# Up projection of a decoder layer: right sums of twelve pairs formed in HBM by DMA, five pairs by seven products in five chunks, and six u tiles kept in HBM

## The chip, the cores and the metric

The kernel runs on one core of one Trainium2 chip. The metric is the time of one execution in microseconds on the device; for the kernel before it is the median of 3 runs. A profile of one execution shows what each engine did: TensorE (PE; its weight loads apart, PEld), VectorE (DVE), ScalarE (ACT), GpSimd (POOL) and SyncE (SP). SP and GpSimd also issue DMAs; each of the two has an order of its own and stands still at an instruction whose semaphores aren't there yet.

## The reference

One layer of a decoder: 256 tokens, width 2048, eight heads of dilated window attention beside eight heads of latent attention, then an MLP of width 8192. All in float32. The change lies in the up projection:

```python
x = x + _rmsnorm(mixed @ w_out[layer], norm_attn_post[layer])
h = _rmsnorm(x, norm_mlp_pre[layer])
u = jnp.square(jax.nn.relu(h @ w_up[layer]))
x = x + _rmsnorm(u @ w_down[layer], norm_mlp_post[layer])
```

## The kernel before

**Precision.** Each float32 operand is split into a part hi and a rest lo, both in a reduced format that TensorE takes; a product of two operands is three matmuls, hi·hi, hi·lo and lo·hi (`three`). Splitting a weight tile is one ScalarE operation (hi, `L306`, or `L310` where a gain is multiplied in) and one VectorE operation (lo, `L307` or `L311`).

**Stages.** Input projections and attention, output projection, residual and norm, up projection, down projection. Weights stream from HBM: `Weights.emit` loads a 512 KB tile into one of 5 raw buffers (on SP's queue), splits it into one of 8 pairs of hi and lo buffers, and runs 6 tiles ahead of the tile in use.

**The up projection** runs over 8 chunks j of 1024 columns of `w_up`. The depth of 2048 is 16 row blocks of 128. A plain step ("k") multiplies one row block with both halves of the tokens and both halves of the columns: 4 products, 12 matmuls. A step by seven products ("w") takes two row blocks (a pair, number kp) and does the 2 x 2 block product with 7 products in place of 8: 21 matmuls where two plain steps take 24. For that it needs sums of the left blocks (`left_sums`, made once, kept in `late["st"]`) and sums of the right, the weights: with the pair's blocks b11, b12 (upper rows) and b21, b22 (lower rows), t holds b11 + b12 and b12 + b22, u holds b11 + b12 + b22 and that plus b21. VectorE makes t and u from the raw pair (`seven`, `L361`, `L365`, `L366`; about the same from two raw tiles, `L364`); four tiles are then split: b11 alone (512 columns), the lower block b (1024), u and t.

A pair's raw weights come as one DMA of 1 MB on GpSimd's queue into the buffer `ab` or `ab2` (`L374`), or as two raw tiles. `UP_STEPS` holds the steps of each chunk: none by seven products in chunk 0, three in chunks 1 and 7, four in chunks 2 to 6, there with a plain step between any two. The products that go to more than one accumulator are gathered in banks m; `close` adds them up in `c` at the chunk's end (`L1043`), and four adds (`L1109`) put that on the accumulators. Each chunk then gives two u tiles (relu and scale, transpose on TensorE, square): `up_evac`, emitted in the next chunk. The 16 u tiles stay in SBUF until the down projection splits them (`split_u`).

**Order.** Nothing is scheduled at run time: the program writes each engine's instructions in one order. A planner (`Flow`) keeps a clock that advances with each matmul written, and chains (generators) that yield delays; `flow.pump` writes the next piece of every chain that is due. The clock decides only where in the order a piece stands.

**GpSimd's queue before.** From the start to the up projection it holds the small power operations of the norms (`L501`: rstd_pre, rstd_kv, rstd_q, rstd_pw, rstd_post) and two or three fills; then the DMAs of the pairs.

Of the kernel before, what the change touches and what calls it, by code (L numbers as in the profile page):

```python
# [98 lines left out]
UP_PAIRS = [()] + [("ab", "ab2", "ab", "ab2")] * 5 + [("ab2", "ab", "raw", "ab"), ("ab", "raw", "raw")]  # L99
# [11 lines left out]
UP_STEPS = [up_steps(range(16)), THREE] + [FOUR] * 5 + [THREE]  # L111

ST = 13 * 256
# [150 lines left out]
def layer(nc, tc, io):  # L264
# [79 lines left out]
    late = {}  # L344
# [32 lines left out]
    def seven_up(j, kp):  # L377
        def load():
            if UP_PAIRS[j][kp] == "raw":
                return [weights.load(up_weight(j, 2 * kp + i), CW, f"raw_w{j}_{kp}{i}") for i in range(2)]  # L380
            return load_two(late[UP_PAIRS[j][kp]], nc.gpsimd if (j, kp) > (1, 0) else nc.sync,
                            io["w_up"][2 * kp * P:(2 * kp + 2) * P, j * CW:(j + 1) * CW])

        return seven(load, lambda: [late["up"].tile([P, CW], F32, tag="T", bufs=2, name=f"{n}{j}_{kp}") for n in "tu"])
# [32 lines left out]
    for j in range(FF // CW):  # L417
        wide_u.append([])
        for what, k in UP_STEPS[j]:
            if what == "k":  # L420

                ts = [weights.plan(up_weight(j, k), 1, CW, *([gcol[:, 8 + k:9 + k]] if j < 2 or k >= 2 * max(N_SEVEN) else []))]
            else:
# [254 lines left out]
    pre = flow.start(prelude())  # L678
    tab = flow.start(tables())
# [253 lines left out]
    def up_evac(j, b, i, acc, order):  # L933
# [8 lines left out]
        if j not in uT:  # L942
            if j in (0, 1, 10, 11, 12, 13):
                t2 = late["u01" if j < 2 else "ab2" if j < 12 else "ab"][:, j % 2 * CW:(j % 2 + 1) * CW]
            else:
                tag = {"tag": "T", "bufs": 2} if j > 13 else {}
                t2 = late["up"].tile([P, CW], F32, name=f"uT{j}", **tag)
            uT[j] = t2.rearrange("p (k s) -> p k s", k=4)
        nc.scalar.activation(uT[j][:, :, b * P:(b + 1) * P], t.rearrange("p (k s) -> p k s", k=4), AF.Square)

# [32 lines left out]
    def left_sums(kp):  # L983
# [9 lines left out]
        keep = kp >= min(N_SEVEN[1:])  # L993
# [5 lines left out]
        st = [late["st"][:, 768 * kp + i * n:768 * kp + (i + 1) * n] for i in range(2)]  # L999
# [8 lines left out]
        yield 0.5  # L1008

# [11 lines left out]
    def seven_products(ts, left, accs, m, first, last, m_first=False):  # L1021
# [6 lines left out]
        for p, (a, i, half, to) in enumerate(prods):  # L1028
            w = weights.get(ts[i])
            in_m = isinstance(to, int)  # L1030
# [20 lines left out]
    for j in range(FF // CW):  # L1051
# [9 lines left out]
        for t, b in order:  # L1061
            what, k, tiles = steps[t]
            if (j, t, b) == (0, 8, 0):
# [4 lines left out]
                late["st"] = late["up"].tile([P, ST], F32R, tag="st", bufs=1, name="st")  # L1068
                for n in ("ab", "ab2", "c", "u01"):
# [5 lines left out]
            if (j, what, k, b) == (1, "k", 8, 0):  # L1075
# [233 lines left out]
```

## Time and profile before

| | us |
|---|---|
| median of 3 runs (1047.1 to 1048.34) | 1047.68 |
| span of the profiled execution, first to last instruction | 1045.7 |
| TensorE busy in the span | 1035.7 |
| VectorE busy | 838.7 |
| ScalarE busy | 630.4 |
| GpSimd busy | 51.5 |
| HBM read / written | 212.72 MB / 15.73 MB |

The span leaves out what lies before the first and after the last instruction. Busy times are shares of one execution. The profile has several views: the page (busy times, 40 slices, DMA queues, the chain of work that ended last, the costliest groups), groups by line, a timeline, waits, and windows (busy time of each engine in a stretch of time). Times in them count from the span's start. A group names its line, engine, operation, output tile, input tiles and shape. In this execution chunk 1 of the up projection begins at 401.4 us, chunk 2 at 444.7 and the down projection at 701.6.

### The profile page before, as it was taken

The page shows a single profiled execution, that of the slowest core. Times are in us where ns is not written, and L with a number is a line of the kernel's source. Part 1 is how long each engine was busy: PE and PEld are TensorE (multiplying, and loading weights), DVE is VectorE, ACT ScalarE, POOL GpSimd, SP SyncE. Part 2 cuts the span into 40 slices and gives each one's busy share as a digit, 9 for nine tenths or more (in the row PEclk, how much of TensorE's full clock was granted, in tenths as well). Part 3 has the DMA queues.
Part 4 walks back from the last instruction along what each step waited for, and adds up shares of the span by engine and source line. Part 5 has one row for each costly group of instructions (what it writes and reads, how often), then busy time and mean ns, then how long its engine had stood idle before and what let it go on. Part 6 is the DMA issues. An engine that isn't in the chain of part 4 may idle for free.

```text
span 1045.7 us, 13378 instructions
## 1 busy us (share of the span) xinstructions
PE 1035.7 (99%) x4837; PEld 863.2 (83%) x4837; DVE 838.7 (80%) x1122; ACT 630.4 (60%) x848; POOL 51.5 (5%) x83
## 2 busy tenths in 40 slices
PE   9999999999999999999999999999999999999996
PEld 6888889888888888888888888888888888888885
DVE  6676536567557669999999999897899978999995
ACT  6674436565545566665765667666567564766661
POOL 0000000000000000000000000000000000111100
PEclk9999999999999999999999999999999999999998
DMA  9975547454447295646657356378778767698952
GB/s 303 370 229 148 140 129 241 146 162 153 150 156 236 92 360 188 216 147 207 202 185 246 121 201 207 113 253 325 274 276 303 265 232 261 238 332 323 356 204 83
DMA packets 79938, 229.33 MB, mean 219 GB/s; under 512 B 6912, under 2 KB 11520, under 8 KB 79488
## 3 DMA queue, kind: packets, MB, share of 16 engines
q1 hardware_dynamic: 64576, 171.47, 48.9%
q0 software_dynamic: 14864, 56.63, 15.2%
q8 instruction: 38, 0.62, 0.3%
q10 hardware_dynamic: 432, 0.37, 0.1%
q14 instruction: 28, 0.23, 0.1%
HBM read 212.72 MB, written 15.73 MB: 218 GB/s over the span
## 4 chain that ended last, share of the span: by engine, by line
PE 97%; DVE 1%; issue 1%; ACT 0%; POOL 0%; DVEq 0%; POOLq 0%; ACTq 0%
PE y L296 25%; PE acc_u L296 24%; PE acc_o L296 8%; PE m L296 7%; PE md L296 5%; PE acc_qk L296 4%; PE acc_v L296 4%; PE acc_ckv L296 2%; PE acc_ukv L296 2%; PE acc_q L296 2%; PE acc_cq L296 2%; PE acc_k L296 2%; PE acc_uq L296 2%; PE rt L300 1%; PE sc_b L296 1%
## 5 line engine op out<-in xcount | busy, mean ns | idle before, releaser
L307 DVE TENSOR_TENSOR lo<-raw,hi 128x1024 fp32r<-128x1024 f32 (+3 forms) x213 | 241.5, 1152 | 89.8 <-ACT hi L306 89.1
L306 ACT ACTIVATE hi<-raw 128x1024 fp32r<-128x1024 f32 (+3 forms) x213 | 209.9, 999 | 73.6 <-PE y L296 16.1
L296 PE MATMUL y<-hi,uhi 128*128 128x512 f32 x370 | 144.4, 390 | 0.0
L296 PE MATMUL y<-hi,ulo 128*128 128x512 f32 x370 | 144.1, 389 | 0.0
L296 PE MATMUL y<-lo,uhi 128*128 128x512 f32 x370 | 144.0, 389 | 0.0
L296 PE MATMUL acc_u<-hi,hT_hi 128*128 128x512 f32 x356 | 141.7, 398 | 0.0
L296 PE MATMUL acc_u<-hi,hT_lo 128*128 128x512 f32 x356 | 139.2, 391 | 0.4 <-DVE hT_lo L307 0.4
L296 PE MATMUL acc_u<-lo,hT_hi 128*128 128x512 f32 x356 | 138.9, 390 | 0.0
L311 DVE SCALAR_TENSOR_TENSOR lo<-raw,gcol,hi 128x1024 fp32r<-128x1024 f32 x74 | 92.5, 1279 | 9.5 <-ACT hi L310 9.5
L310 ACT ACTIVATE hi<-raw,gcol 128x1024 fp32r<-128x1024 f32 x74 | 83.7, 1148 | 25.0 <-DMA raw<-in_w_up 11.7
L296 PEld LDWEIGHTS y<-hi,ulo 128*128 128x128 f32 x370 | 69.5, 188 | 14.4
L296 PEld LDWEIGHTS y<-lo,uhi 128*128 128x128 f32 x370 | 69.5, 188 | 14.3
L296 PEld LDWEIGHTS y<-hi,uhi 128*128 128x128 f32 x370 | 69.5, 188 | 14.2
L296 PEld LDWEIGHTS acc_u<-hi,hT_lo 128*128 128x128 f32 x356 | 66.8, 188 | 14.9 <-DVE hT_lo L307 0.8
L296 PEld LDWEIGHTS acc_u<-lo,hT_hi 128*128 128x128 f32 x356 | 67.0, 188 | 12.8
L296 PEld LDWEIGHTS acc_u<-hi,hT_hi 128*128 128x128 f32 x356 | 67.0, 188 | 12.8
L306 ACT ACTIVATE hi<-u 128x1024 fp32r<-128x1024 f32 (+1 forms) x38 | 37.4, 990 | 49.2 <-DVE u L366 35.4
L307 DVE TENSOR_TENSOR lo<-st_down,hi 128x1024 fp32r<-128x1024 f32 x42 | 50.4, 1220 | 3.0 <-ACT hi L306 2.8
L296 PE MATMUL acc_o<-hi,mixT_hi 128*128 128x512 f32 x128 | 51.8, 405 | 0.0
L306 ACT ACTIVATE hi<-st_down 128x1024 fp32r<-128x1024 f32 x42 | 43.9, 1052 | 12.6 <-PE y L296 9.5
L296 PE MATMUL acc_o<-hi,mixT_lo 128*128 128x512 f32 x128 | 50.2, 392 | 0.0
L296 PE MATMUL acc_o<-lo,mixT_hi 128*128 128x512 f32 x128 | 50.0, 391 | 0.0
(328 smaller groups left out, 2087.7 us busy)
## 6 DMA issues: line engine op xcount, KB each, us to landing
raw<-in_w_down SPq DMA_DIRECT2D x86, 512.0 KB, 5.8
raw<-in_w_up SPq DMA_DIRECT2D x76, 512.0 KB, 4.6
raw<-in_w_in SPq DMA_DIRECT2D x55, 512.0 KB, 4.9
ab<-in_w_up POOLq DMA_DIRECT2D x22, 1024.0 KB, 5.4
raw<-in_w_out SPq DMA_DIRECT2D x32, 512.0 KB, 4.2
ab_down<-in_w_down POOLq DMA_DIRECT2D x11, 1024.0 KB, 7.1
ukeep<-ulo SPq DMA_DIRECT2D x15, 512.0 KB, 7.0
ulo<-ukeep POOLq DMA_DIRECT2D x15, 512.0 KB, 6.2
```

Of the source, the lines that this page charges most:

```text
L296: nc.tensor.matmul(out, a, b, start=start, stop=stop)
L300: nc.tensor.transpose(out, a, ident)
L306: nc.scalar.activation(hi, src, AF.Copy)
L307: nc.vector.tensor_tensor(out=lo, in0=src, in1=hi.bitcast(F32), op=OP.subtract)
L310: nc.scalar.activation(hi, src, AF.Copy, scale=g)
L311: nc.vector.scalar_tensor_tensor(out=lo, in0=src, scalar=g, in1=hi.bitcast(F32), op0=OP.mult, op1=OP.subtract)
```

## The change

**Right sums by DMA.** `MADE` names twelve pairs (chunk, pair): pair 1 in chunks 1 and 7, pairs 1 and 3 in chunks 2 to 6. A new chain `make_sums`, started at the beginning with a delay of 62 and steps of 4.8 on the planner's clock, writes four DMAs for each on GpSimd's queue, in batches of three pairs: a copy of the pair from `w_up` to a new HBM tensor (1 MB), an add of b12 and b22 onto b11 and b12 (512 KB), an add of b22 onto b21 (256 KB), and an add of the first sum onto the second half (512 KB, from the tensor itself). The adds are DMAs that accumulate. In the up projection these pairs are four ordinary weight tiles on SP's queue (512, 1024, 1024 and 1024 columns; two of them from the made tensor), and VectorE makes no sums for them.

**More pairs.** Chunks 2 to 6 take five pairs in place of four, chunk 7 four in place of three: six pairs more. The steps of chunks 2 to 6 are now blocks 10 to 13, pairs 0, 1, block 14, pairs 2, 3, 4, block 15. A fifth set of left sums is made in chunk 1 (`two_sums`), in a tile `st4`; `late["st"]` shrinks by 256 columns.

**u tiles in HBM.** The raw pairs that aren't made use `ab` and `ab2` alone, through chunk 7 too, so these no longer hold u tiles 10 to 13. The u tiles 2 to 7 are stored to HBM on SP's queue 6 units after they are written (`u_away`, in chunks 2 to 4), their buffers serve tiles 8 to 13, and they are read back: 2 and 3 in chunk 7, 4 to 7 at the start of the down projection.

How this moves instructions on VectorE, in chunk 4, from the splits of pair 2 to the last plain block. Before (lo is the rest of a split tile, t and u the sums of the pair named after them, raw a loaded tile):

```order
L307 TENSOR_TENSOR lo_4964<-ab,hi_4963 128x1024
L307 TENSOR_TENSOR lo_4971<-u_2_4931,hi_4970 128x1024
L307 TENSOR_TENSOR lo_4981<-t_2_4930,hi_4980 128x1024
L361 TENSOR_TENSOR t_3_4991<-ab_3503 128x1024
L365 TENSOR_TENSOR u_3_4992<-t_3_4991,ab_3503 128x512
L366 TENSOR_TENSOR u_3_4992<-u_3_4992,ab_3503 128x512
L311 SCALAR_TENSOR_TENSOR lo_4999<-raw_4996,gcol,hi_4998 128x1024
L307 TENSOR_TENSOR lo_5009<-ab_3503,hi_5008 128x512
L307 TENSOR_TENSOR lo_5025<-ab_3503,hi_5024 128x1024
L307 TENSOR_TENSOR lo_5032<-u_3_4992,hi_5031 128x1024
L307 TENSOR_TENSOR lo_5042<-t_3_4991,hi_5041 128x1024
L311 SCALAR_TENSOR_TENSOR lo_5054<-raw_5051,gcol,hi_5053 128x1024
```

Now, from the splits of pair 3, which is made in HBM, to those of pair 4:

```order
L309 TENSOR_TENSOR lo_5085<-raw_5082,hi_5084 128x512
L309 TENSOR_TENSOR lo_5097<-raw_5094,hi_5096 128x1024
L386 TENSOR_TENSOR t_4_5113<-ab 128x1024
L390 TENSOR_TENSOR u_4_5114<-t_4_5113,ab 128x512
L391 TENSOR_TENSOR u_4_5114<-u_4_5114,ab 128x512
L309 TENSOR_TENSOR lo_5121<-raw_5118,hi_5120 128x1024
L309 TENSOR_TENSOR lo_5130<-raw_5127,hi_5129 128x1024
L309 TENSOR_TENSOR lo_5140<-ab,hi_5139 128x512
L309 TENSOR_TENSOR lo_5150<-ab,hi_5149 128x1024
L309 TENSOR_TENSOR lo_5160<-u_4_5114,hi_5159 128x1024
L309 TENSOR_TENSOR lo_5167<-t_4_5113,hi_5166 128x1024
L313 SCALAR_TENSOR_TENSOR lo_5179<-raw_5176,gcol,hi_5178 128x1024
```

The plain block's split between the pairs is gone, and pair 3 comes as four raw tiles without sums of its own.

GpSimd's queue ahead of the output projection's norms, before (the power operations, and a fill):

```order
L501 TENSOR_TENSOR rstd_kv<-t_kv,neg_half 128x2
L501 TENSOR_TENSOR rstd_q<-t_q,neg_half 128x2
L738 MEMSET krT 128x512
L501 TENSOR_TENSOR rstd_pw<-t_pw,neg_half 128x2
L501 TENSOR_TENSOR rstd_post_3197<-t_post_3196,neg_half 128x1
```

Now, the last batch (made_1_79, made_3_80 and made_1_81 are the tensors of pairs 1 and 3 of chunk 6 and of pair 1 of chunk 7):

```order
L368 DMA made_1_79<-in_w_up 128x2x512
L368 DMA made_1_79<-in_w_up 128x512
L368 DMA made_3_80<-in_w_up 128x2x512
L368 DMA made_3_80<-in_w_up 128x512
L368 DMA made_1_81<-in_w_up 128x2x512
L368 DMA made_1_81<-in_w_up 128x512
L368 DMA made_1_79<-made_1_79 128x2x512
L528 TENSOR_TENSOR rstd_pw<-t_pw,neg_half 128x2
L368 DMA made_3_80<-made_3_80 128x2x512
L368 DMA made_1_81<-made_1_81 128x2x512
L528 TENSOR_TENSOR rstd_post_3257<-t_post_3256,neg_half 128x1
```

Of the 48 new DMAs 20 stand ahead of rstd_kv, 5 between it and rstd_q, 21 between that and rstd_pw, and 2 behind rstd_pw; the adds wait for the copies and for the adds that they build on.

The diff, its core:

```diff
-UP_PAIRS = [()] + [("ab", "ab2", "ab", "ab2")] * 5 + [("ab2", "ab", "raw", "ab"), ("ab", "raw", "raw")]
+MADE = [(), (1,)] + [(1, 3)] * 5 + [(1,)]
+D_MADE, MADE_STEP, MADE_BATCH = 62.0, 4.8, 3
...
-UP_STEPS = [up_steps(range(16)), THREE] + [FOUR] * 5 + [THREE]
-
-ST = 13 * 256
+FIVE = up_steps(range(10, 14), (), (14,), (), (), (15,))
+UP_STEPS = [up_steps(range(16)), THREE] + [FIVE] * 5 + [FOUR]
+
+ST = 12 * 256
...
+    def make_sums():
+
+        jobs, add = [(j, kp) for j in range(FF // CW) for kp in MADE[j]], {"accum_op": OP.add}
+        H = 512
+        yield D_MADE
+        for i in range(0, len(jobs), MADE_BATCH):
+            todo = [[], [], []]
+            for j, kp in jobs[i:i + MADE_BATCH]:
+                s = made[j, kp]
+                w = up_pair(j, kp).rearrange("(k p) n -> p k n", k=2)
+                todo[0].append((s.rearrange("p (k n) -> p k n", k=2), w, {}))
+                todo[1].append((s[:, :CW].rearrange("p (k n) -> p k n", k=2), w[:, :, H:], add))
+                todo[1].append((s[:, CW:CW + H], w[:, 1, H:], add))
+                todo[2].append((s[:, CW:].rearrange("p (k n) -> p k n", k=2), s[:, :H].unsqueeze(1).to_broadcast([P, 2, H]), add))
+            for group in todo:
+                for out, src, kw in group:
+                    nc.gpsimd.dma_start(out=out, in_=src, **kw)
+                    yield MADE_STEP
...
+            elif k in MADE[j]:
+                s = made[j, k] = dram.tile([P, 2 * CW], F32, name=f"made{j}_{k}")
+                ts = [weights.plan(up_weight(j, 2 * k)[:, :512], 1, 512), weights.plan(up_weight(j, 2 * k + 1), 1, CW),
+                      weights.plan(s[:, CW:], 1, CW), weights.plan(s[:, :CW], 1, CW)]
...
     pre = flow.start(prelude())
+    flow.start(make_sums())
...
+        if b and 2 <= j < 8:
+            flow.start(u_away(j), 6.0)
+
+    U_HOME = {2: 8, 3: 9, 10: 4, 11: 5, 12: 6, 13: 7}
+    uaway = {}
+
+    def u_away(j):
+        uaway[j] = dram.tile([P, CW], F32, name=f"uaway{j}")
+        nc.sync.dma_start(out=uaway[j], in_=uT.pop(j).rearrange("p k s -> p (k s)"))
+        yield 0
+
+    def u_back(j, t):
+        nc.sync.dma_start(out=t, in_=uaway[j])
+        uT[j] = t.rearrange("p (k s) -> p k s", k=4)
...
-            if (j, what, k, b) == (1, "k", 8, 0):
-                fourth = flow.start(left_sums(3), 20.0)
-            if j == 2 and t == 0:
-                flow.finish(fourth)
+            if (j, what, k, b) == (1, "k", 10, 0):
+                more_sums = flow.start(two_sums(), 12.0)
+            if (j, what, k) == (1, "w", 2):
+                flow.finish(more_sums)
+            if (j, t, b) == (FF // CW - 1, 6, 0):
+                for i in (2, 3):
+                    u_back(i, late["up"].tile([P, CW], F32, tag=f"k{i}", bufs=1, name=f"uT{i}_back"))
...
+    for i in range(4, 8):
+        u_back(i, late["ab" if i < 6 else "ab2"][:, i % 2 * CW:(i % 2 + 1) * CW])
```

35 lines of the change are left out of this document (22 added, 13 removed).

## The prediction

> **What bounds the kernel now.** I read the page's busy times and chain of waits first, then the chain in time order over the up projection, then VectorE's groups there, then the windows of the DMA engines.
>
> ```profile
> span 1045.7 us, 13378 instructions
> PE 1035.7 (99%) x4837; PEld 863.2 (83%) x4837; DVE 838.7 (80%) x1122; ACT 630.4 (60%) x848; POOL 51.5 (5%) x83
> ...
> PE 97%; DVE 1%; issue 1%; ACT 0%; POOL 0%; DVEq 0%; POOLq 0%; ACTq 0%
> ```
>
> TensorE is busy for 1035.7 of 1045.7 us and is 97% of the chain that ended last. So a matmul taken out shortens the kernel by its own pace, as long as nothing else becomes late. The chain in time order gives that pace (start, length, piece):
>
> ```profile
> 482.78 9.52 PE acc_u L296 x42
> ...
> 520.04 2.72 PE acc_u L296 x12
> 522.76 2.72 PE m L296 x12
> 525.48 9.52 PE acc_u L296 x42
> ```
>
> Twelve products in 2.72 us are 0.2267 us each. The 390 ns that the page gives for one product is its length in the pipeline, not its pace. Chunks start 42.70 us apart (482.78 and 525.48 are the same place in two of them), and 180 products at 0.2267 us are 40.8 us of that; sixteen transposes and their joints are the rest. VectorE stands right behind. Its groups in one chunk (line, operation, shape, count; busy us and mean ns; idle before them):
>
> ```profile
> L311 DVE SCALAR_TENSOR_TENSOR lo<-raw,gcol,hi 128x1024 fp32r<-128x1024 f32 x8 | 9.9, 1279 | 0.0
> L307 DVE TENSOR_TENSOR lo<-t,hi 128x1024 fp32r<-128x1024 f32 x4 | 4.9, 1220 | 0.8 <-ACT hi L306 0.8
> ...
> L361 DVE TENSOR_TENSOR t<-ab 128x1024 f32<-128x1024 f32 x4 | 4.9, 1218 | 0.0
> ...
> L365 DVE TENSOR_TENSOR u<-t,ab 128x512 f32<-128x512 f32 x4 | 2.8, 692 | 0.1
> L307 DVE TENSOR_TENSOR lo<-ab,hi 128x512 fp32r<-128x512 f32 x4 | 2.7, 686 | 0.3 <-ACT hi L306 0.3
> L1043 DVE TENSOR_TENSOR c<-m,c 128x512 f32<-128x512 f32 x4 | 2.7, 688 | 0.2
> L1109 DVE TENSOR_TENSOR acc_u<-acc_u,c 128x512 f32<-128x512 f32 x4 | 2.5, 692 | 0.0
> ```
>
> ```profile
> 444.68:487.38 42.70, 42.70 (x198) 35.35 (x196) 40.87 (x44) 28.08 (x33) 2.85 (x4) 1.00 0.62 203
> ```
>
> The second row is the same chunk as a window: TensorE 42.70 of 42.70 us, VectorE 40.87 (the means, with those of the rows left out, which repeat these, overlap and add to 43.5, so I scale sums of them by 0.94). VectorE has 1.83 us of slack per chunk. This is the stage in which the change must be judged.
>
> **The products.** A pair by seven products takes 21 matmuls where two plain row blocks take 24. Five chunks go from four pairs to five and the last from three to four: six pairs, 18 matmuls, 18 x 0.2267 = 4.08 us. That is the whole gain.
>
> **VectorE and ScalarE in a chunk.** Two plain splits go (2 x 1.279), one sum of t and u goes (1.218 + 2 x 0.692 = 2.60; three of five pairs still make theirs), and one pair's splits come (0.686 + 3 x 1.220 = 4.35). Together -0.81 us by the means, against -0.68 us on TensorE: VectorE keeps its share, 96%. The danger is the order: pairs 2, 3 and 4 now follow each other with no plain block between. In that run VectorE needs 3 x 4.35 + 2 x 2.60 = 18.3, scaled 17.2 us, and TensorE only 63 x 0.2267 = 14.3. So it loses 2.9 us of lead. What lead it has, I count from the chunk's start:
>
> ```profile
> 487.40 2.49 DVE L1109 TENSOR_TENSOR acc_u<-acc_u,c 128x512 f32<-128x512 f32 x4
> ...
> 519.59 1.22 DVE L307 TENSOR_TENSOR lo<-t,hi 128x1024 fp32r<-128x1024 f32 x1
> 520.73 6.06 DVE L311 SCALAR_TENSOR_TENSOR lo<-raw,gcol,hi 128x1024 fp32r<-128x1024 f32 x5
> ```
>
> The four adds of the accumulators end 2.4 us after TensorE starts the chunk (487.40 is that start). Then come the sums of pairs 0 and 2, the rest of pair 0, pairs 1 and 2 and one plain block: 2 x 2.60 + 3.66 + 2 x 4.35 + 1.28 = 18.8, scaled 17.7, plus 0.8 of waiting as in the row of lo<-t. Pair 2's last tile is ready at 20.9; TensorE reaches it after 117 products and the transposes, at 28.3. That lead of 7.4 us falls to some 4.5 in pair 4. Before, the smallest lead is that of pair 3: its t tile is ready at 519.59 + 1.22 = 520.8, and TensorE, which starts that pair at 522.76, wants it six products later, at 524.1: 3.3 us. The new minimum isn't smaller, so I cost the order at nothing; ScalarE issues the same splits and has more room.
>
> Chunk 1 gets one block of left sums more:
>
> ```profile
> 429.46 0.69 DVE L989 TENSOR_TENSOR c<-hT_hi,hT_lo 128x512 f32<-128x512 f32 x1
> ...
> 435.78 0.69 DVE L1005 TENSOR_TENSOR st<-c,st 128x512 fp32r<-128x512 f32 x1
> ```
>
> These are the first and the last of nine such operations, 3.8 us together, less the 2.6 of one sum: 1.2 us of lead, and up to 1 us more because it waits for ScalarE's halves in the middle. The 3.3 us cover it; uncovered it costs 2.
>
> **The DMA work on GpSimd's queue.** The 48 new DMAs, 12 copies of 1.05 MB and 36 adds, move 28.3 MB. The program spaces them 4.8 us apart, but GpSimd doesn't know that clock: it issues until it stands at an instruction that waits. These are its markers:
>
> ```profile
> 62.62 0.71 POOL L501 TENSOR_TENSOR rstd_pre<-t_pre,neg_half 128x2 f32<-128x2 f32 x1 [61.28 <-DVE t_pre L500]
> 180.84 0.70 POOL L501 TENSOR_TENSOR rstd_kv<-t_kv,neg_half 128x2 f32<-128x2 f32 x1 [117.51 <-DVE t_kv L500]
> 205.72 0.69 POOL L501 TENSOR_TENSOR rstd_q<-t_q,neg_half 128x2 f32<-128x2 f32 x1 [24.18 <-DVE t_q L500]
> ...
> 319.20 1.69 POOL L501 TENSOR_TENSOR rstd_pw<-t_pw,neg_half 128x2 f32<-128x2 f32 x1 [112.32 <-DVE t_pw L500]
> ```
>
> So 20 DMAs (12.3 MB, 6.0 of it adds) go out as fast as they land from 62.6 us on, and then GpSimd stands at rstd_kv until 180.8; 20 more (11.0 MB, 6.8 adds) fall between about 207 and rstd_pw at 319.2. What room the DMA engines have there (window and length, PE, PEld, DVE, ACT, POOL, clock, DMA share, GB/s):
>
> ```profile
> 62.60:180.80 118.20, 118.20 (x645) 103.31 (x644) 68.40 (x134) 62.71 (x107) 0.71 (x1) 1.00 0.57 173
> ...
> 206.90:319.20 112.30, 112.11 (x573) 96.15 (x572) 72.32 (x156) 65.15 (x127) 0.00 (x1) 1.00 0.50 163
> ...
> 950.00:975.00 25.00, 25.00 (x112) 20.72 (x111) 23.15 (x27) 17.85 (x20) 3.00 (x5) 1.00 0.99 373
> 700.00:725.00 25.00, 25.00 (x120) 20.71 (x119) 21.12 (x25) 16.87 (x21) 1.43 (x2) 1.00 0.95 354
> ```
>
> ```profile
> q0 software_dynamic: 14864, 56.63, 15.2%
> ```
>
> The software queue moved 56.63 MB in 15.2% of 1045.7 us: 356 GB/s. Free are 0.43 x 118.2 = 50.8 us and 0.50 x 112.3 = 56.2 us. No row shows an add. Its floor is a load's price: 34.6 and 30.9 us. Its ceiling I set at three times a load (read the source, read the target, write): 68.5 and 69.3 us. I take twice, since the copy's nearest rows (a 512 KB write to HBM lands in 7.0 us, a load in 4.6) lie nearer one than three:
>
> ```profile
> raw<-in_w_up SPq DMA_DIRECT2D x76, 512.0 KB, 4.6
> ...
> ukeep<-ulo SPq DMA_DIRECT2D x15, 512.0 KB, 7.0
> ```
>
> Twice gives 51.6 and 50.1 us: they just fit. What they cost is then only what they take from the weight loads, and those run ahead: TensorE has eight split tiles, and the SP queue mostly stands waiting for a buffer (waited for; us in total, times, longest):
>
> ```profile
> SPq L190 <- DVE lo L307: 39.2, 16, 5.8
> ```
>
> In the window from 950 us both queues ran the engines at 0.99 and 373 GB/s with TensorE at 25.00 of 25, so a full DMA engine alone stops nothing. Cost 0; from a loss of 20 us at the ceiling (below) to nothing at the floor, since nothing there could bring a gain.
>
> The Trainium skill, page "DMA: Bandwidth & Descriptors", section "Queues, rings and completion order", says that a DMA engine takes turns between the queues it has work for, one packet at a time. By that rule a slow add packet between any two load packets sets what is left for the loads; with adds at twice the sum stays at 1043.6, with adds at three times it becomes the first rival. No run so far shows two queues with unequal packets.
>
> **What waits behind a late add.** rstd_kv, rstd_q and rstd_pw stand behind adds. Their readers:
>
> ```profile
> 210.04 0.47 ACT L807 ACTIVATE kb<-acc_ukv,rstd_kv 128x256 f32<-128x256 f32 x1
> ```
>
> ```profile
> 320.92 0.17 DVE L850 TENSOR_SCALAR pw<-rstd_pw 128x2 int32<-128x2 int32 x1 [0.58 <-POOL rstd_pw L501]
> ```
>
> rstd_kv would have to be 28 us late (180.8 + 0.7 to 210.0) to hold ScalarE. rstd_pw is read at once, and VectorE's splits queue behind it; TensorE's lead there is the full eight tiles, since ScalarE waits for a tile to come free:
>
> ```profile
> 320.74 1.06 ACT L306 ACTIVATE hi<-raw 128x1024 fp32r<-128x1024 f32 x1 [1.66 <-PE acc_o L296]
> ```
>
> Eight tiles at 2.72 us are 21.8 us of cover. The second burst at the ceiling needs 69.3 us in 56.2 free ones, 13 late. Cost 0. A GpSimd issue takes the 0.7 us of the rows for ab, and nobody waits for it.
>
> **The u tiles.** Six stores on SP wait for the square of the tile:
>
> ```profile
> 499.63 0.60 ACT L949 ACTIVATE uT<-rt 128x512 f32<-128x512 f32 x1 [0.84 <-PE rt L300]
> ```
>
> That square ends 12.9 us into the chunk; the load behind it would have gone at about 10, when pair 1's first split frees its buffer. It is held 2.9 us and is wanted 11 us after it could go, against 4.6 to landing and 1.06 to split: hidden. At the start of the down projection 2.1 MB come back when the engines are 0.95 busy (the 700 us row): 6 us of loads, under the lead of the split tiles. The first tiles back are asked for half a chunk ahead. Cost 0, bound 6.
>
> **Sum.** 1045.7 - 4.08 = 1041.6 for the profiled span. The median lies 1.98 us above the span, so 1043.6.
>
> **The rivals.**
> First, the loads starve, and it is slower. If an add packet takes three times a load's, the loads get a quarter of 356, 89 GB/s, against the 173 and 163 that the windows need, for 68.5 / 0.75 = 91 us in the first burst and 92 in the second. Missing are 7.6 and 6.8 MB; eight split tiles and half of the five raw buffers hold 5.5. TensorE waits 2.1 MB / 173 = 12 us and 1.3 / 163 = 8: 1043.6 + 20 = 1064. It decides once the loads fall below 113 GB/s, 32% of the engines. For it: no add is in the trace, and the first burst meets the 0.57 window. Against: the 950 us window, and a lead that was full.
> Second, VectorE becomes the bound. It has 40.1 us of work and 1.8 of waits in a chunk of 42.0; if the tiles that come as loads bring 0.8 us of waits (what lo<-t shows for one pair), the period is 42.7 as before, and only chunk 7's 0.68 is left: 1047.0. For it: the 96%. Against: a lead of 4.5 us.
> Third, the stores hold SP: three chunks that lose the 2.9 us each, 1043.6 + 8.6 = 1052. Against: the cover just counted.
> Fourth, the change takes out more than I say: were a product worth its 390 ns, 18 would be 7.0 us, 1040.6. The pace row speaks against it.
>
> **How the numbers follow.** Forecast 0.60, first rival 0.17, second 0.12, third 0.07, fourth 0.04. A measurement of this kernel tells about 0.2%, 2.1 us, from no change. Faster is the forecast and the fourth, 0.64; same the second, 0.12; slower 0.24. The forecast's own range is 1042.6 to 1045.4 (half a microsecond of pace, 2 us of chunk 1). To hold 8 in 10 it must reach the second and third rivals, and a mild first one: 1042.4 to 1052.5.
>
> **What would show it.** After: 18 matmuls fewer; the chunks of five pairs 42.0 us apart with TensorE full, and VectorE near 40; the made copies and adds ended before rstd_kv and rstd_pw, and those two at 181 and 319 as before; DMA share near 1 from 63 us on, without TensorE idle there. ScalarE's hi waiting for raw<-in_w_in at 65 to 160 us, or for raw<-in_w_out up to 319, would prove the first rival; ScalarE's hi waiting for raw<-made, the second; hi waiting for raw behind uaway in chunks 2 to 4, the third. If rstd_pw comes over 20 us late, I have mispriced the adds.

## The result, and the profile after

The changed kernel takes 1084.77 us (median of 4 runs, 1080.83 to 1088.28) against 1047.97 for the kernel before: 1.035 times as long, with a 95% interval from 1.033 to 1.038. The forecast was 1043.6 with a range up to 1052.5, so the change went the other way, by far. The profiled execution has a span of 1082.6 us, 36.9 more than before. Its page begins:

```profile
span 1082.6 us, 13538 instructions
...
PE 1042.8 (96%) x4819; PEld 862.3 (80%) x4819; DVE 836.4 (77%) x1122; ACT 636.5 (59%) x862; POOL 96.0 (9%) x128
...
PE 57%; DVE 21%; DMA 12%; issue 5%; ACT 4%; POOL 0%; DVEq 0%; POOLq 0%; ACTq 0%; SPq 0%
...
L308 ACT ACTIVATE hi<-raw 128x1024 fp32r<-128x1024 f32 (+3 forms) x261 | 253.7, 990 | 161.7 <-DMA raw<-in_w_in 60.4
```

The 18 matmuls are gone (4819 against 4837). But TensorE, 97% of the chain of waits before, is 57% now; VectorE and DMA transfers hold most of the rest. The last row is ScalarE's halves of the weights: of 161.7 us of waiting 60.4 are for loads of w_in. Where the 36.9 us arose is read from places that both traces have: the first ab tile on GpSimd's queue at 398.35 us (377.46 before), the first add to the accumulators at the end of chunk 1 at 468.21 (444.56), of chunk 6 at 691.26 (658.62), of chunk 7 at 735.11 (701.24), and rstd_fin at 1069.72 (1033.20). So:

| Stretch | lost, us | forecast |
|---|---|---|
| start to the first ab tile | 20.9 | 0 |
| from there to the end of chunk 1 | 2.8 | 0 |
| chunks 2 to 6 (five pairs) | 9.0 | -3.4 |
| chunk 7 (four pairs) | 1.2 | -0.7 |
| down projection | 2.7 | 0 |

There are three places, and each has its own row. First the stretch of the DMAs, in windows (window and length, then busy us of TensorE, its weight loads, VectorE, ScalarE, GpSimd, then clock, DMA share, GB/s); the last row is one chunk of five pairs:

```profile
62.60:127.00 64.40, 55.91 (x257) 45.02 (x255) 32.71 (x69) 28.64 (x47) 19.59 (x21) 0.97 1.04 296
127.00:193.20 66.20, 65.43 (x390) 59.29 (x391) 36.66 (x68) 33.98 (x61) 0.15 (x1) 1.00 0.71 209
219.00:282.00 63.00, 57.94 (x300) 50.35 (x299) 39.71 (x92) 33.41 (x66) 20.19 (x22) 0.95 1.06 290
282.00:340.60 58.60, 58.60 (x280) 48.33 (x278) 32.53 (x64) 31.59 (x62) 0.47 (x1) 1.00 0.68 211
512.84:557.48 44.64, 42.57 (x195) 34.58 (x194) 40.09 (x44) 29.05 (x35) 2.15 (x3) 1.00 0.73 252
```

The DMAs go out in two bursts of some 62 us in which the DMA engines are full (1.04 and 1.06) and TensorE stands for 8.5 and 5.1 us by its records; between them the engines have room again (0.71, 0.68) and nothing is left to issue. GpSimd's timeline (start, length, instruction, and in brackets how long it stood and for whom) says the same:

```profile
193.21 0.73 POOL L528 TENSOR_TENSOR rstd_kv<-t_kv,neg_half 128x2 f32<-128x2 f32 x1 [66.06 <-DVE t_kv L527]
...
340.61 1.63 POOL L528 TENSOR_TENSOR rstd_pw<-t_pw,neg_half 128x2 f32<-128x2 f32 x1 [58.13 <-DVE t_pw L527]
```

It had issued all it could and stood 66 and 58 us for VectorE. rstd_kv is 12.4 us late and rstd_pw 21.4, and not because adds held them up: they wait for a late TensorE. What TensorE waits for stands in the list of its own waits in the whole execution (for whom: us in total, times, longest); these five rows lie in the two bursts:

```profile
PE pT_a L302 <- DVE s_a L659: 4.1, 2, 2.9
PE sc_a L298 <- DVE qkT_a L683: 2.9, 2, 2.2
PE qrt L302 <- DVE qr L640: 2.5, 1, 2.5
PE o_a L298 <- ACT pT_a L665: 2.3, 1, 2.3
PE pT_b L302 <- DVE s_b L659: 1.9, 1, 1.9
```

All are steps of the attention, and no row of that list is for a split weight tile: TensorE did not run out of those. The attention's steps stand in ScalarE's and VectorE's order behind the halves of weight tiles whose loads are not there, as here (ScalarE, then VectorE):

```profile
93.10 1.06 ACT L308 ACTIVATE hi<-raw 128x1024 fp32r<-128x1024 f32 x1 [1.99 <-DMA raw<-in_w_in]
```

```profile
94.19 1.23 DVE L309 TENSOR_TENSOR lo<-raw,hi 128x1024 fp32r<-128x1024 f32 x1 [2.69 <-ACT hi L308]
...
95.53 0.55 DVE L659 TENSOR_SCALAR s_a<-s_a,st_a 128x128 f32<-128x128 f32 x2
```

TensorE's transposes of that s_a start at 95.96, after the longest of these waits, 2.9 us. With a sixth row of 0.6 these waits add up to 14.3 of the 21.4 us. Most of the rest comes right behind three of them: from 96 to 99, 253 to 256 and 277 to 280 us TensorE's granted clock is 0.50, which costs some 1.5 us each time.

Why the loads are late shows in the DMA view from 65 to 127 us, queue by queue (packets, MB, share of 16 engines) and load by load (count, KB, median us to landing). After:

```profile
q0 software_dynamic: 3976, 10.78, 67.3%
q1 hardware_dynamic: 3986, 7.69, 37.5%
...
raw<-in_w_in SPq DMA_DIRECT2D x16, 512.0 KB, 18.5
```

and the same window before:

```profile
q1 hardware_dynamic: 5256, 10.18, 55.0%
...
raw<-in_w_in SPq DMA_DIRECT2D x17, 512.0 KB, 4.0
```

A weight load lands after 18.5 us instead of 4.0. The loads get 7.69 MB in 62 us, 124 GB/s, where TensorE needed 10.18 MB, 164 GB/s. Five raw buffers of 0.524 MB, each held 18.5 us by its load and some 2.6 by its two halves (1.06 and 1.22 us, and the joints), give 2.62 / 21.1 = 124 GB/s: an estimate that meets the measured rate. It says that all buffers were in use, not that their number was the limit: the two queues moved the same number of packets, so the loads' queue seems to have had one ready at every turn, and with more buffers the landing may only have taken longer. No run changed their number.

Second, a chunk of five pairs: its adds come 44.63 us apart, not 42.0. VectorE's work is as forecast (40.09 us), but it stands 4.1 us at the chunk's start. ScalarE's timeline there, and then VectorE's three waits, show for whom:

```profile
517.99 1.06 ACT L308 ACTIVATE hi<-u 128x1024 fp32r<-128x1024 f32 x1 [3.74 <-DVE u L391]
518.95 0.67 ACT L965 ACTIVATE r<-acc_u,rstd_pre 128x512 f32<-128x512 f32 x1
...
520.00 1.06 ACT L308 ACTIVATE hi<-t 128x1024 fp32r<-128x1024 f32 x1
...
521.43 1.28 ACT L965 ACTIVATE r<-acc_u,rstd_pre 128x512 f32<-128x512 f32 x2
522.57 0.65 ACT L308 ACTIVATE hi<-raw 128x512 fp32r<-128x512 f32 x1
...
524.73 0.60 ACT L978 ACTIVATE uT<-rt 128x512 f32<-128x512 f32 x1 [1.02 <-PE rt L302]
525.22 2.95 ACT L308 ACTIVATE hi<-raw 128x1024 fp32r<-128x1024 f32 x3
```

```profile
521.09 1.23 DVE L309 TENSOR_TENSOR lo<-t,hi 128x1024 fp32r<-128x1024 f32 x1 [0.79 <-ACT hi L308]
...
523.25 0.69 DVE L309 TENSOR_TENSOR lo<-raw,hi 128x512 fp32r<-128x512 f32 x1 [0.94 <-ACT hi L308]
...
526.31 2.36 DVE L309 TENSOR_TENSOR lo<-raw,hi 128x1024 fp32r<-128x1024 f32 x2 [2.36 <-ACT hi L308]
```

The halves of pair 1's three large tiles (hi<-raw at 525.22) stand behind the last square of the old chunk (uT at 524.73), this behind TensorE's transposes, these behind the second r at 518.95, and that behind hi<-u, which waited 3.74 us for VectorE's sums. Before, pair 1's sums on VectorE (2.6 us) stood at that place, so it had work. Third, the down projection; its rows come with its experiment.

### The profile page after: what moved, and what is told of

It reads as the page before. It is cut to its first block, busy times and chain, and to the rows that moved or that the text cites. A ratio compares the mean times of both kernels' runs of the same rounds, so it can differ in the third digit from the quotient of the medians.

```text
span 1082.6 us, 13538 instructions
## 1 busy us (share of the span) xinstructions
PE 1042.8 (96%) x4819; PEld 862.3 (80%) x4819; DVE 836.4 (77%) x1122; ACT 636.5 (59%) x862; POOL 96.0 (9%) x128
## 4 chain that ended last, share of the span: by engine, by line
PE 57%; DVE 21%; DMA 12%; issue 5%; ACT 4%; POOL 0%; DVEq 0%; POOLq 0%; ACTq 0%; SPq 0%
PE y L298 24%; DVE lo L309 9%; DMA raw<-in_w_in 8%; PE acc_o L298 7%; PE acc_u L298 7%; PE md L298 5%; DVE lo L313 4%; DMA raw<-in_w_out 3%; PE acc_ckv L298 2%; ACT hi L308 2%; PE acc_cq L298 2%; PE acc_v L298 2%; DVE t L386 2%; DVE acc_u L1163 1%; PE acc_ukv L298 1%
## 5 line engine op out<-in xcount | busy, mean ns | idle before, releaser
L309 DVE TENSOR_TENSOR lo<-raw,hi 128x1024 fp32r<-128x1024 f32 (+3 forms) x261 | 292.0, 1139 | 145.8 <-ACT hi L308 145.2
L308 ACT ACTIVATE hi<-raw 128x1024 fp32r<-128x1024 f32 (+3 forms) x261 | 253.7, 990 | 161.7 <-DMA raw<-in_w_in 60.4
L298 PE MATMUL acc_u<-hi,hT_hi 128*128 128x512 f32 x320 | 128.3, 401 | 1.5 <-DVE c L1093 1.5
L298 PE MATMUL acc_u<-hi,hT_lo 128*128 128x512 f32 x320 | 125.2, 391 | 0.4 <-DVE hT_lo L309 0.4
L298 PE MATMUL acc_u<-lo,hT_hi 128*128 128x512 f32 x320 | 124.8, 390 | 0.0
L313 DVE SCALAR_TENSOR_TENSOR lo<-raw,gcol,hi 128x1024 fp32r<-128x1024 f32 x62 | 77.2, 1278 | 13.0 <-ACT hi L312 13.0
L312 ACT ACTIVATE hi<-raw,gcol 128x1024 fp32r<-128x1024 f32 x62 | 69.6, 1145 | 13.3 <-DMA raw<-in_w_up 9.3
L298 PEld LDWEIGHTS acc_u<-hi,hT_hi 128*128 128x128 f32 x320 | 60.1, 188 | 14.9 <-DVE c L1093 3.6
L298 PEld LDWEIGHTS acc_u<-hi,hT_lo 128*128 128x128 f32 x320 | 60.0, 188 | 13.8 <-DVE hT_lo L309 0.9
L298 PE MATMUL m<-hi,st 128*128 128x512 f32 x138 | 51.9, 389 | 0.0
```

What stands on the lines that cost most here:

```text
L298: nc.tensor.matmul(out, a, b, start=start, stop=stop)
L308: nc.scalar.activation(hi, src, AF.Copy)
L309: nc.vector.tensor_tensor(out=lo, in0=src, in1=hi.bitcast(F32), op=OP.subtract)
L312: nc.scalar.activation(hi, src, AF.Copy, scale=g)
L313: nc.vector.scalar_tensor_tensor(out=lo, in0=src, scalar=g, in1=hi.bitcast(F32), op0=OP.mult, op1=OP.subtract)
```

## The experiments

Each time is of one execution, except in the last two runs, which have ten; the kernel before took 1048.0 to 1048.9 us beside them. Markers of each in us: rstd_kv, rstd_pw, the first add at the end of chunk 1, the mean distance of the adds from the end of chunk 2 to that of chunk 5, and the time.

| Run | rstd_kv | rstd_pw | end of chunk 1 | chunk | time |
|---|---|---|---|---|---|
| before | 180.84 | 319.20 | 444.56 | 42.70 | 1047.97 |
| after | 193.21 | 340.61 | 468.21 | 44.63 | 1084.77 |
| e1 before + DMAs | 195.48 | 344.19 | 469.32 | 42.70 | 1072.22 |
| e2 before + copies | 192.44 | 336.49 | 461.39 | 42.70 | 1064.32 |
| e3 after - DMAs | 181.06 | 319.74 | 447.47 | 44.63 | 1063.22 |
| e4 e3, pairs 2 and 4 | 180.69 | 319.21 | 447.14 | 45.39 | 1068.59 |
| e5 e3, three tiles ahead | 181.01 | 319.72 | 445.62 | 43.57 | 1057.00 |
| e6 e3, four pairs | 181.24 | 319.71 | 443.67 | 43.20 | 1051.42 |
| e7 e1, paced 9 us | 182.24 | 324.49 | 471.42 | 54.7 | 1137.82 |
| e8 e3, u back late | 182.31 | 321.03 | 448.70 | 44.64 | 1062.01 |
| e9 e1, paced 6 us | 180.93 | 323.04 | 446.98 | 42.70 | 1050.19 |
| e10 e5, close evacuations | 181.14 | 319.77 | 445.70 | 42.01 | 1045.22 |
| e11 after, all edits | 182.17 | 324.19 | 449.16 | 42.00 | 1047.72 |
| e12 e11, paced 5.5 us | 181.38 | 322.34 | 452.31 | 42.00 | 1050.91 |

**The DMAs alone.** Into the kernel before go the scratch tiles in HBM, make_sums unchanged, and its start:

```diff
+    made = {(j, kp): dram.tile([P, 2 * CW], F32, name=f"made{j}_{kp}") for j in range(FF // CW) for kp in MADE[j]}
...
     pre = flow.start(prelude())
+    flow.start(make_sums())
```

> The kernel before, with the 48 copying and adding DMAs of the change on GpSimd's queue and nothing else of it; what they make is not read. Theory (the loss ahead of the up projection, 20.9 us at the first ab tile of the changed kernel, is these DMAs against the weight loads): rstd_kv at about 193 and rstd_pw at about 340 as in the changed kernel, up chunks 42.7 us apart, time 1047.7 + 21 = 1069. Rival (the early loss needs something else of the change, for example the moved pools): rstd_pw at 319, time 1048.

In the second, the adds are plain copies of the same shapes, which leaves the sums out:

```diff
-{"accum_op": OP.add}
+{}
```

> As the run with the DMAs alone, but each of the 36 adding DMAs is a plain copy of the same shape, so that the sums are not made. Theory A (the accumulation is what is dear): copies at a load's price of 356 GB/s fit the free engine time, time 1048 to 1052. Theory B (bytes and bursts are what is dear, an add costs about what a copy from HBM to HBM costs): within 5 us of the run with the DMAs alone, 1064 to 1069. The landing times in the changed kernel (copies 14.4 us, adds of the same size 14.9) speak for B.

The DMAs alone cost 24.2 us at the end (1048.0 beside them to 1072.22): the first part of the loss is theirs. Plain copies still cost 16.3. That time lies in B's range, but 7.9 us under e1 and not within 5: the adding itself does cost. (The landing times named for B compare copies of 1024 KB with adds of 512 KB, so they spoke for neither.) The page's row of the software queue prices both, of e1 (span 1070.5) and then of e2 (span 1062.5):

```profile
q0 software_dynamic: 26384, 84.94, 26.6%
```

```profile
q0 software_dynamic: 22544, 84.94, 23.1%
```

Less the 158.9 us of before (15.2% of 1045.7), the 28.3 MB took 125.8 us of the engines with adds and 86.5 as copies. Copies go at 327 GB/s, 1.09 times the price of a load; at that price the 12.6 MB of real copies are 38.4 us, and the 15.7 MB of adds take 87.4 us, 180 GB/s: 2.0 times a load. That is the price that the prediction took. And e2, near the floor price, starves the loads all the same; in its DMA view from 65 to 127 us stands:

```profile
raw<-in_w_in SPq DMA_DIRECT2D x17, 512.0 KB, 16.4
```

While they last, copies leave the loads about what adds leave them: 126 GB/s from 100 to 115 us in e2, where the queues moved 982 and 1038 packets, and 134 from 85 to 110 us in the changed kernel, with 1736 and 1653. But they are done sooner: GpSimd stands 78.5 us at rstd_kv, 67.5 in e1. What costs is the burst first, and the adds make it longer.

**Pacing them.** Ahead of each DMA GpSimd reads two columns of the split tile that was issued last, so that it cannot run ahead of the program:

```diff
-D_MADE, MADE_STEP, MADE_BATCH = 62.0, 4.8, 3
+D_MADE, MADE_STEP, MADE_BATCH = 62.0, 9.0, 3
...
                 for out, src, kw in group:
+                    l = weights.tiles[-1][1]
+                    l = l[:, 0, :2] if len(l.shape) == 3 else l[:, :2]
+                    nc.gpsimd.tensor_tensor(out=pace, in0=l.bitcast(F32), in1=l.bitcast(F32), op=OP.mult)
                     nc.gpsimd.dma_start(out=out, in_=src, **kw)
```

> The kernel before with the same 48 copying and adding DMAs as in the run with the DMAs alone, unread; but ahead of each one GpSimd multiplies two columns of the split tile that was issued last (into a scratch of its own), so that it cannot issue before the program has got there, and they are spaced 9 us apart in the program instead of 4.8: 62 to about 490 us. Theory (the bursts are what starves the loads; 28.3 MB at 1.6 times a load's price are 127 us of the DMA engines, in 430 us of which about half are free): no loss beyond 3 us, 1048 to 1051. Rival (each add slows the loads it meets, however spaced): 10 us or more, 1058 to 1072.

1137.82 us, worse than anything. But up to rstd_post (349.91 against 348.50) this run had lost 1.4 us with 28 of the 48 DMAs out. It lost the rest in chunks 0 to 4, and the waits of GpSimd and VectorE in the whole execution (for whom: us in total, times, longest; con_pad is the scratch of the markers) show why:

```profile
POOL con_pad L370 <- DVE lo L309: 320.6, 32, 20.2
```

```profile
DVE t L390 <- DMA ab<-in_w_up: 66.2, 8, 10.1
```

GpSimd stood at its markers, 137.3 of the first row's us from 349 us on, with the ab loads of the pairs queued behind it, and VectorE waited for those. So the same edit with 6.0 for 9.0, which puts the last DMA, at 402.3 us, ahead of the first ab load:

> As the run with the DMAs paced at 9 us, but 6 us apart, so that all 48 are issued by about 370 us, ahead of the first chunk of the up projection that has ab loads: there the paced run had lost some 85 us, since GpSimd stood at its markers with the ab loads queued behind it; up to 350 us it had lost only 1.4. Theory (bursts starve the loads, spacing does not, and the 85 us are the markers): rstd_post at 349 to 353, chunks 42.7 us apart, time 1049 to 1054. Rival (the adds lose what they cost wherever they are; 48 in the time in which 32 cost 1.4 us fill the DMA engines): rstd_post at 360 or later, 1060 or more.

1050.19: the theory holds. The same 84.94 MB take as long in the engines (27.8% of 1048.1 us, 132 us above before, against 125.8), but between 62 and 349 us, with 41 of the 48 out, nothing is lost (rstd_post at 348.71, 348.50 before). Loads of w_in land in 5.7 us, and TensorE has no wait of over 0.3 us for a step of the attention. The rival falls.

**The chunks without the DMAs.** The made tiles are loaded from rows of w_up, so the right sums of the twelve pairs are left out:

```diff
-                      weights.plan(s[:, CW:], 1, CW), weights.plan(s[:, :CW], 1, CW)]
+                      weights.plan(up_weight(j, 2 * k), 1, CW), weights.plan(up_weight(j, 2 * k + 1), 1, CW)]
...
-    flow.start(make_sums())
```

> The changed kernel without the 48 DMAs: the tiles of the twelve pairs are loaded from rows of the up weights with the same bytes, so their right sums are left out of the computation. Theory (the early loss of 21 us is the DMAs; the 9.5 us of the five chunks with five pairs, the 2.8 of chunk 1 and the 3.7 of the start of the down projection are not): first ab tile at 377, chunks 44.6 us apart, time 1084.8 - 21 = 1064. Rival (the DMAs' loss is all, the chunks are slow because the made tiles come late from HBM): chunks 42.0 us apart, time 1044.

1063.22, as the theory said, and 44.63 us a chunk to the hundredth as in the changed kernel. So the chunks' loss has nothing to do with the DMAs. Then the loaded pairs were moved:

```diff
-MADE = [(), (1,)] + [(1, 3)] * 5 + [(1,)]
+MADE = [(), (1,)] + [(2, 4)] * 5 + [(1,)]
```

> As the run without the 48 DMAs, with pairs 2 and 4 instead of 1 and 3 as the loaded ones in the five chunks, so that VectorE again makes the sums of pair 1 itself at the start of a chunk; the same instructions otherwise. Theory (VectorE stands empty at the start of a chunk, because pair 1's splits wait for ScalarE's halves and those stand behind the evacuation of the chunk before; sums of pair 1 would fill that time): the chunks go from 44.6 to 42.0 to 42.7 us apart, 10 to 13 us less than the run without the DMAs, about 1052. Rival (VectorE has too much to do wherever the pairs lie, or the accumulators' adds come too late): 44 us or more, within 3 us of that run.

My theory fell: 1068.59, chunks 45.39 us apart. VectorE's waits in the chunk from 585.4 us, all of them:

```profile
593.68 1.23 DVE L309 TENSOR_TENSOR lo<-t,hi 128x1024 fp32r<-128x1024 f32 x1 [0.79 <-ACT hi L308]
598.88 1.23 DVE L309 TENSOR_TENSOR lo<-ab,hi 128x1024 fp32r<-128x1024 f32 x1 [0.78 <-ACT hi L308]
622.30 5.13 DVE L313 SCALAR_TENSOR_TENSOR lo<-raw,gcol,hi 128x1024 fp32r<-128x1024 f32 x4 [2.92 <-ACT hi L312]
```

The wait at the start did shrink, from 4.1 to 1.6 us, and 2.9 came at the end, where ScalarE waited 4.0 us for TensorE to free a split tile. Giving VectorE something to do isn't enough; the chunk is a ring through three engines. That ring was the next theory, and its edit is one number, which issues the splits of the next chunk later against the adds and the evacuation:

```diff
             if last:
-                weights.ahead -= 1
+                weights.ahead -= 3
```

> As the run without the 48 DMAs (1063.2), but from the last pair of a chunk on, splits are issued only three tiles ahead instead of five, so that VectorE closes the products and adds to the accumulators two plain splits earlier, and ScalarE's halves of pair 0's sums stand behind all four evacuations of the old chunk instead of ahead of three. The same instructions, another order. Theory (the chunk is a ring: VectorE's adds to the accumulators, sums of pair 0, ScalarE's half of u, its evacuation behind that, TensorE's transposes and products, VectorE's splits; 4.1 us of VectorE's wait in it are due to that order): the ring shortens by 2 us or more, chunks 42.0 to 42.7 us apart, time 1050 to 1054. Rival (VectorE's work in a chunk of five pairs doesn't fit, in whatever order): chunks 44 us or more apart, time within 3 us of 1063.

43.57 us a chunk and 1057.00: half of what the theory expected, and against the rival too. The chain of waits of e5 shows what was left (the pieces where it leaves TensorE and comes back to it):

```profile
543.77 0.45 PE rt L302 x4
...
544.25 0.03 ACT uT L977
...
544.74 1.06 ACT hi L308
...
568.24 1.23 DVE lo L309
...
569.51 1.45 PE m L298 x5
```

From the last transposes on VectorE needs 25 us up to pair 4's t tile, and TensorE waits for it. What starts this stretch is the last square, so the evacuations were moved closer together:

```diff
-                evac.append(flow.start(up_evac(2 * j + n, b, at[b, n], accs[b, n], o + 0.6)))
+                evac.append(flow.start(up_evac(2 * j + n, b, at[b, n], accs[b, n], 0.5 * o + 0.6)))
```

> As the run with splits only three tiles ahead (1057.0, chunks 43.6 us apart), with the four evacuations 1.1 us apart in the program instead of 2.2, so that ScalarE's halves of u and t of pair 0 stand behind all four and TensorE's last transposes come some 3 us earlier. Theory (VectorE, held until the last square is done, then has 23.7 us of splits and sums up to pair 4's t tile against TensorE's 24: a start 2 to 3 us earlier frees TensorE): chunks 42.0 to 42.6 us apart, time 1050 to 1053. Rival (VectorE's work doesn't fit in any order): chunks 43.3 or more, within 2 us of 1057.

42.01 us a chunk: the forecast's 42.0, with every instruction of e3 and nothing but their order changed. 1045.22 is 18 us under e3 and better than expected. ScalarE's rows of that run, at the place shown above:

```profile
534.41 0.69 ACT L964 ACTIVATE r<-acc_u,rstd_pre 128x512 f32<-128x512 f32 x1 [1.63 <-PE rt L302]
...
538.46 0.60 ACT L977 ACTIVATE uT<-rt 128x512 f32<-128x512 f32 x1 [0.35 <-PE rt L302]
538.95 1.05 ACT L308 ACTIVATE hi<-u 128x1024 fp32r<-128x1024 f32 x1
539.90 1.05 ACT L308 ACTIVATE hi<-t 128x1024 fp32r<-128x1024 f32 x1
540.85 3.46 ACT L308 ACTIVATE hi<-raw 128x512 fp32r<-128x512 f32 x4
```

The last square comes 8.2 us after the first add (538.46 against 530.27), where it was 11.9 in the changed kernel (524.73 against 512.84). All evacuations are ahead of hi<-u, and the halves of pair 1 run through without a gap. TensorE holds the whole chain from 480 to 650 us again:

```profile
by line: PE acc_u L298 62.7%; PE m L298 33.4%; PE rt L302 4.1%
```

The last of this group takes the fifth pair away again and keeps two loaded ones (and doesn't make the fifth block of left sums):

```diff
-UP_STEPS = [up_steps(range(16)), THREE] + [FIVE] * 5 + [FOUR]
+UP_STEPS = [up_steps(range(16)), THREE] + [FOUR] * 5 + [THREE]
```

> As the run without the 48 DMAs, but with four pairs in the five chunks and three in the last, as in the kernel before; pairs 1 and 3 are still loaded, and the fifth block of left sums is not made. VectorE has two sums of t and u (5.2 us by the means) less to do in each chunk than in the kernel before. Theory (it is VectorE's load and order that set the period): chunks 42.7 us apart as in the kernel before, the end of chunk 1 at 445, and what is left is the start of the down projection: 1047.7 + 3.4 = 1051. Rival (loaded pairs cost more than made ones anywhere, since their tiles come by SP's queue and all their halves stand behind the evacuation): chunks 44 us or more apart, 1058 or more.

The total is as expected, 1051.42, its parts only roughly: chunks of 43.2 us instead of 42.7, and 1.2 us lost in the down projection instead of 3.4. The rival's 44 us and 1058 are missed, but something of it stays: the five chunks are longer than before although VectorE has only 36.5 us of work in them, so with this order loaded pairs cost a little even where VectorE has room. It isn't VectorE's load alone. The end of chunk 1 at 443.67, 3.8 us under e3, shows chunk 1's loss to be the fifth left sums; e5 got 1.9 of its 2.9 us back by order alone.

**The down projection.** In e3 the SP queue issues, and the chain of waits there reads:

```profile
706.39 2.05 SPq L990 DMA_DIRECT2D ab<-uaway  x4
708.54 18.08 SPq L192 DMA_DIRECT2D raw<-in_w_down  x9
```

```profile
709.17 9.27 DMA raw<-in_w_down
```

```diff
-    for i in range(4, 8):
-        u_back(i, late["ab" if i < 6 else "ab2"][:, i % 2 * CW:(i % 2 + 1) * CW])
+    def backs():
+        for i in range(4, 8):
+            u_back(i, late["ab" if i < 6 else "ab2"][:, i % 2 * CW:(i % 2 + 1) * CW])
+            yield 6.0
+
+    flow.start(backs(), 10.0)
```

> As the run without the 48 DMAs (1063.2), but the four u tiles that come back at the start of the down projection are asked for 10, 16, 22 and 28 us into it instead of all at once ahead of its first weights. Theory (2.1 MB in front of the first weights of the down projection on SP's queue hold them 5.9 us at 356 GB/s; the start of the down projection lost 3.4 us): time 1063.2 - 3.4 = 1060. Rival (the engines are full there, whoever comes first; or the wait comes from the late last chunk): within 1 us of 1063.2.

1062.01: 1.2 us less, a third of what was expected, on one run each. This run stood 1.25 us behind e3 at rstd_kv already and 2.9 at the end of chunk 7, both ahead of what the edit moves, and from there to rstd_fin it took 330.12 us against 334.21. So in its own stretch the edit took away the whole loss, with VectorE as late as in e3. In e10, with the tiles back at once but VectorE in time, that stretch took 332.92 (331.96 before): that took away most of it too. It seems to need both; but e5, whose chunks were faster than e3's, took 335.43, and single executions don't settle how it divides.

**All together.** The changed kernel, whole, with the pacing at 6 us, the two numbers of the order, and the late u tiles:

> The changed kernel, whole, with the three edits together: the 48 DMAs paced 6 us apart by GpSimd's markers, splits three tiles ahead with the evacuations 1.1 us apart, and the four u tiles asked for late. By the terms: 1047.7, 0 to 5 for the DMAs, 1 for chunk 1, -3.4 for the five chunks at 42.0 (or 0 at 42.7), -0.7 for the last chunk, 1 to 2 left at the start of the down projection: 1046 to 1054. Theory (the three losses are separate and add): in that range, at most 0.6% over the kernel before, over 30 us under the changed one. Rival (they are one loss, VectorE's, and the mends of the early part come back later): 1060 or more.

1047.72 us (10 runs) against 1048.16 (13 runs): a ratio of 1.0001, from 0.9992 to 1.0011. The time is in the range that the theory gave, so the losses can be mended one by one, and the mended change is worth nothing. Its windows of the attention part and of chunks 0 and 1:

```profile
62.00:182.00 120.00, 120.00 (x652) 104.67 (x651) 69.66 (x137) 63.11 (x108) 19.26 (x33) 1.00 0.87 256
...
350.00:450.00 100.00, 97.88 (x452) 79.91 (x451) 81.35 (x118) 60.74 (x85) 15.03 (x21) 1.00 0.83 250
```

TensorE is full up to 182 us with the DMA engines at 0.87. By the adds, chunks 2 to 7 bring 4.8 us (251.88 against 256.68), chunk 1 ends 4.6 us late and the down projection takes 0.6 more: what the products bring goes again ahead of chunk 2, where e10, without the DMAs, was 1.1 us late. The other 3.5 are the DMAs' or chance.

> As the run with all three edits (1047.7), the DMAs 5.5 us apart instead of 6, so that the last adds fall some 20 us earlier and fewer of them meet the loads of chunk 0 of the up projection. What is left in that run over the one without the 48 DMAs (1045.2) is 2.5 us, lost between 349 and 449 us, where ScalarE waits for raw<-in_w_up. Theory (the adds that run on into chunk 0 take that time): 1 to 2 us less, 1045.5 to 1047. Rival (the DMA engines, busy 0.82 to 0.87 in the attention part, have no more room there): 1047.5 to 1051.

1050.91 us (10 runs), a ratio of 1.0024 from 1.0015 to 1.0034: the theory fell, and the time is the rival's. Its reason isn't shown: rstd_post comes at 348.94 us (349.89 in e11), so nothing was lost in the attention part. The chunks stay at 42.00, and in the profiled execution, the slowest of the ten, chunk 1 ends 3.2 us later than with 6 us. So no whole version here beats the kernel before by what a measurement can tell, and how the DMAs meet the loads of chunk 0 in detail stays open.

## Why the prediction was wrong, step by step

**What bounds the kernel, and the pace.** Right. The chunk of 42.0 us was measured in e10, e11 and e12. The gain of the products is real, and in e11 it is 4.8 us with chunk 7.

**VectorE in a chunk.** The work was right (40.09 us against "near 40"). The step that failed is "ScalarE issues the same splits and has more room", with "plus 0.8 of waiting as in the row of lo<-t": it took ScalarE's free time for its order, and carried the wait of one row over to an order in which another instruction stood behind it. The waits were 4.1 us; the 0.79 at lo<-t is the one foreseen, the other 3.3 stand at pair 1's tiles. The lead of 7.4 falling to 4.5 us wasn't there, since VectorE started pair 1 after the last square and not from the chunk's start. The second rival named this bound and gave it 42.7 us; it was 44.63, because the wait runs round the ring and isn't only VectorE's. Its sign, ScalarE's hi waiting for raw<-made, did not show, and e3 has the same chunks without made tiles. Chunk 7 had the same and lost 1.2 where 0.7 was to be won.

**Chunk 1.** The size was nearly right ("uncovered it costs 2", measured 2.8), the cover of 3.3 us wasn't there: e6 without the fifth left sums doesn't lose it.

**The DMA work.** The price was right (2.0 times a load), and so was that they go out as fast as they land. (The second burst has 21 DMAs and 12.1 MB, not 20 and 11.0; at twice that is 53.0 us, still under the 56.2.) Two steps failed after that. I set the engine time of a burst, 51.6 us, against the free time of the whole stretch to rstd_kv, 50.8 of 118; a burst takes its time at once, and within 62 us it left the loads 124 of 164 GB/s. And "those run ahead: TensorE has eight split tiles" put the cost of late loads at nothing. The cover was to be 5.5 MB, and the loads were only 10.18 - 7.69 = 2.5 MB short when TensorE had lost most of its 12.4 us. It had split tiles; what it lacked were the steps of the attention behind the halves of late tiles, 14.3 us of waits in the two bursts. Tiles ahead don't cover those. The window from 950 us, where full engines stop nothing, was no evidence: there both queues bring what TensorE needs, and here one of them brought what nobody needed for 200 us.

The first rival gave 12 + 8 = 20 us and 12.4 + 9.0 were measured up to rstd_pw, but not by its mechanism. It needed adds at three times a load, loads below 113 GB/s and a TensorE without split tiles; the loads got 124, e2 starved them with copies at 1.09 times, and TensorE waited for other things. The sign that I had set for a mispriced add, rstd_pw over 20 us late, came true with the price right. A better sign was in the prediction too: ScalarE's hi waiting for raw<-in_w_in, which stood at those 60.4 us.

The Trainium skill, page "DMA: Bandwidth & Descriptors", section "Queues, rings and completion order", has a DMA engine take turns between queues packet by packet. The trace agrees as far as its counts go: 3976 and 3986 packets of the two queues in the 62 us shown above. The rule doesn't need dear packets to do harm, and there I weighed it wrongly.

**What waits behind a late add.** Right as far as it went: nothing waited for an add. **The u tiles.** The stores are free, as said: chunks 5 and 6 have none and are as far apart as chunks 2 to 4. Getting them back was under its bound of 6 (2.7 us in that stretch, and e8 and e10 don't settle how much of it is VectorE's).

**The chances.** I gave the first rival 0.17 and the second 0.12 as if one excluded the other. They lie in different stages, and the loss of each came, if not by its mechanism. Together they gave 1064 + 3.4 = 1067, which the range didn't reach either.

## What to carry to other kernels

Set the engine time of a background transfer against the room in the time in which it is really issued, not in the stretch in which it is allowed; a queue without an instruction to wait at runs in bursts. Tiles ahead cover only a late tile: in a fixed order, a split that waits for its load also holds up whatever stands behind it on its engine, here steps of the attention that TensorE needed at once. Before counting on the lead of an engine that is 96% busy, read which instruction of another engine stands ahead of its next input in the new order, and follow that round until it comes back. Where the same instructions in another order are worth 2.6 us of 44.6, try the order before adding work to save products.

## What was not expected of the hardware

Adding DMAs from HBM to HBM took 2.0 times the engine time of a load (180 GB/s of the bytes added against 356), plain copies 1.09 times (327). Two busy queues moved the same number of packets in the same 62 us (3976 and 3986), and a 512 KB load that landed in 4.0 us then landed in 18.5. Behind waits of 2.9, 2.5 and 1.9 us TensorE ran for some 3 us at a granted clock of 0.50. Spread over some 300 us, the same DMAs took as much engine time (132 us against 126) and cost the loads 0.8 (w_in) to 2.7 us (w_out) in landing and the kernel 2.
